# Loading the first 24 peer_u tiles of a two-layer PEER decoder without a turn on TensorE

## The chip, the cores and the metric

One core of a Trainium2 chip runs the whole kernel. The metric is the device time in microseconds from the start of the program to its end; less is better. Engines are called TensorE (PE in the profile; PEld is its weight load), VectorE (DVE), ScalarE (ACT), GpSimd (POOL) and SyncE (SP), which issues most transfers.

## The reference

Two layers, 256 tokens, 1024 channels. Each layer has a block of two token mixers and a PEER block; the change touches only the PEER block:

```python
q = (h @ w_pq).reshape(B, S, PEER_HEADS, 2, half)
s1 = jnp.einsum('bshd,hnd->bshn', q[..., 0, :], sub_keys[0])
s2 = jnp.einsum('bshd,hnd->bshn', q[..., 1, :], sub_keys[1])
v1, i1 = lax.top_k(s1, PEER_TOPK)
v2, i2 = lax.top_k(s2, PEER_TOPK)
cand = v1[..., :, None] + v2[..., None, :]
top, pos = lax.top_k(cand, PEER_TOPK)        # 16 of 16 x 16 pairs, with their indices idx
gates = jax.nn.softmax(top, axis=-1)
...
act = jax.nn.gelu(jnp.einsum('btd,bthkd->bthk', hb, u), approximate=False)   # u = peer_u[idx]
y = jnp.einsum('bthk,bthkd->btd', gb * act, peer_v[ib])
```

There are 8 heads, 128 keys on either side and so 16384 experts, of which each token and head uses 16. peer_u and peer_v have one row of 1024 channels for each expert.

## The kernel before

The kernel gathers nothing. It goes through all 16384 experts in 128 tiles of 128: for each it multiplies the peer_u tile with the modulated activations of all 256 tokens (hTh and hTl), applies gelu, multiplies by a gate that is zero where a token didn't choose the expert, and adds the products with the peer_v tiles in PSUM. So that float32 inputs keep their precision, each operand is split in a high part (wh, hTh; written by ScalarE) and a rest (wl, hTl), and each product is three: high by high, high by rest, rest by high. A peer_u tile is 8 channel blocks times 3, 24 products.

For a product on TensorE the channels must lie on the partitions, so a peer_u tile is turned. Line 124 names two ways, a kind for each tile:

- Kind u: four transfers (line 197) lay the tile down so that VectorE's block transpose (line 220, in `turn`) finishes the turn. ScalarE then writes the two halves of wh from it, and GpSimd subtracts to get those of wl (line 271, in `prep`).
- Kind x: four transfers (line 193) lay it down otherwise; TensorE turns it by eight transposes of 128x128 into PSUM (line 251, in `prep`), and ScalarE copies each of two banks twice: to wh, and back into the raw tile, from which GpSimd's subtraction reads.

Before, of the first 100 tiles every fourth (3, 7, 11, ...) is of kind x, 25 in a layer.

`take` hands out the tile that is prepared, starts a new transfer, prepares the next tile and turns the one after that. wh and wl have room for two tiles (HALVES), the raw tiles five buffers (RAW). For each tile `u_tile` (lines 1631 to 1643) calls `take`, issues the 24 products and, every second tile, the gelu of the pair before (`fin_u`).

Beside that runs the side work: a generator, `select`, that finds the top 16 and places the gates. After each tile `pull` (line 1650) advances it by a budget. The numbers that the generator yields, called points here, are the author's costs of its steps in microseconds of VectorE; `pull` subtracts them from a credit that it carries on, of at most two budgets, and a yield of None ends the pull of that tile. Every engine does its own work in the order of the program, so the budget sets how many operations of VectorE stand between two transposes. A tile of kind u gets 1.55 points, a tile of kind x 2.75.

The side work has three parts:
- The top-k: 17 steps of `zipped` (lines 1433 to 1438). A round, as it is called below, is one head and one half of the tokens: the key operations (ten, 0.2 points each) of round i interleaved with the candidate operations (0.0, twice 0.12, five times 0.18) of round i - 1. Before each, `scores(i + 1)` issues the score product (tile K) on TensorE and a copy of it on ScalarE; then ScalarE copies the high keys of round i - 1 into PSUM (vp, tile G), and the additions on VectorE (line 1404) read that copy.
- The tail of the selection (lines 1447 to 1498): indices of the chosen pairs, by comparisons and reductions over 2048 elements (lines 1473 to 1478) and many operations over 128.
- The gate placement (`place_gates`): 64 blocks of four tokens, each with two operations of 1024 elements on VectorE (lines 1507 and 1512), products on TensorE, and a product of the gates with the gelu values (line 1539).

After tile 125 `drain` (line 1653) empties what side work is left; then come the last two tiles of peer_u and the peer_v tiles.

Of the kernel before, what the change touches and what calls it, by code (L numbers as in the profile page):

```python
# [24 lines left out]
NK = 128  # L25
# [20 lines left out]
def trunk_kernel(ctx: ExitStack, tc: tile.TileContext, x, c, w_ada, b_ada, w_in, lb_logits, hg_norm_g,  # L46
# [74 lines left out]
            order.append((kind, w[l][k * P:(k + 1) * P, :], 0))  # L121


    uv_seq = [("x" if j % 4 == 3 and j < 100 else "u", j) for j in range(NK)] + [("v", j) for j in range(NK)]
    for l in range(DEPTH):
        if l == 0:

# [507 lines left out]
    def pull(sides, budget):  # L635

        credit[0] = min(credit[0] + budget, 2 * budget)
        for g in list(sides):
            while credit[0] > 0:
                try:  # L640
                    cost = next(g)
                except StopIteration:
                    sides.remove(g)
                    break
                if cost is None:
                    break
                credit[0] -= cost
                load["vector"] += cost
# [670 lines left out]
    def peer(l, hT):  # L1319
        with ExitStack() as es:  # L1320
# [11 lines left out]
            with ExitStack() as eu:  # L1332
# [227 lines left out]
                sides = []  # L1560
# [70 lines left out]
                def u_tile(j):  # L1631
                    h, lo = take(uv_seq[j][0])
                    if j % 2 == 0:
                        acts[0] = pst.tile([P, 2, S], F32, name="A")
                    ps = acts[0]
                    for k0 in (0, KC // 2):
                        kss = [(k, slice(k * P, (k + 1) * P)) for k in range(k0, k0 + KC // 2)]
                        products([(ps[:, j % 2], (h(ks), lo(ks)), (hTh[:, k], hTl[:, k]), k == 0, k == KC - 1)
                                  for k, ks in kss], 0)
                    if pend:  # L1640
                        fin_u(*pend.pop())
                    if j % 2 == 1:
                        pend.append((j - 1, ps))
# [3 lines left out]
                    f()  # L1647
                for i, (kind, j) in enumerate(uv_seq[:nu]):
                    u_tile(j)
                    pull(sides, 1.55 + 1.2 * (kind == "x"))  # L1650
                if pend:
                    fin_u(*pend.pop())
                drain(sides)
# [111 lines left out]
    for l in range(DEPTH):  # L1765
        hT = mixers(l, hT)
        hT = peer(l, hT)
# [27 lines left out]
```

## Time and profile before

| | us |
|---|---|
| median of 3 runs (lowest to highest) | 2228.16 (2227.01 to 2228.52) |
| the profiled execution | 2227.97 |
| its span, first to last instruction | 2226.2 |
| TensorE busy | 2117.0 |
| VectorE busy | 1819.4 |
| ScalarE busy | 1164.5 |
| GpSimd busy | 1063.8 |

The span is 1.8 us shorter than the execution. Busy times are averages over stages that differ: what binds a stage is read from a table by stretches, and who waits for whom from the waits of the stretch. Times of single operations in a timeline are durations; on VectorE one operation can start before the one ahead of it has ended, so the cost of an operation in a full stretch is read from the distance of two starts. In a chain or a timeline, rows of equal kind that follow one another are merged and counted (x24).

### The profile page before, as it was taken

To read this page: it belongs to the slowest core of one execution; us is meant where nothing else is said; L and a number is where in the kernel's file an instruction comes from. 1 tells how busy PE (TensorE), PEld (TensorE's weight loads), DVE (VectorE), ACT (ScalarE), POOL (GpSimd) and SP (SyncE) were. 2 spreads that over 40 slices of the span, in tenths; PEclk is the share of its full clock that TensorE was granted. 3 is DMA by queue.
4 is the path that set the end of the run, shared out by engine and by line. 5 is a ranking of instruction groups with operands and counts; after the bars stand their busy time and mean duration, and the time that the engine had idled before them with its cause. 6 is when DMAs were issued, how large, how long until landed. Compare 5 with 4: busy or idle time off the path is not lost.

```text
span 2226.2 us, 42039 instructions
## 1 busy us (share of the span) xinstructions
PE 2117.0 (95%) x14484; PEld 1928.0 (87%) x14484; DVE 1819.4 (82%) x3296; ACT 1164.5 (52%) x2443; POOL 1063.8 (48%) x784
## 2 busy tenths in 40 slices
PE   5799899999999999999989998998999999999998
PEld 5789799999999977888779887998999999788886
DVE  7887979999999578888887658789999985766675
ACT  3446555545554545555545465555555545555562
POOL 4656637887778621000044534578877783300001
PEclk8899999999999999999999999999999999999999
DMA  8646567676665678888844335676766556666662
GB/s 281 193 133 221 167 132 158 149 151 146 143 147 146 186 251 270 282 283 284 298 153 146 120 103 146 149 155 142 154 146 145 147 159 192 220 196 191 197 226 87
DMA packets 448718, 400.30 MB, mean 180 GB/s; under 512 B 234576, under 2 KB 395896, under 8 KB 448504
## 3 DMA queue, kind: packets, MB, share of 16 engines
q1 hardware_dynamic: 446760, 392.33, 62.5%
q0 software_dynamic: 1408, 4.23, 0.6%
q8 instruction: 114, 1.87, 0.3%
q10 hardware_dynamic: 336, 1.06, 0.1%
q14 instruction: 100, 0.82, 0.1%
HBM read 396.46 MB, written 1.05 MB: 179 GB/s over the span
## 4 chain that ended last, share of the span: by engine, by line
PE 69%; DVE 15%; DMA 5%; issue 3%; ACT 3%; POOL 2%; SPq 1%; POOLq 0%; ACTq 0%; DVEq 0%
PE Y L61 27%; PE A L61 25%; PE T L61 7%; PE G L61 3%; DMA raw<-in_peer_u_dram 3%; POOL wl L271 2%; PE hs L61 2%; DVE wl L271 2%; PE ss L61 2%; PE T L251 2%; DMA raw<-in_peer_v_dram 1%; DVE qk L857 1%; DVE o L1512 1%; SPq L197 1%; DVE e L843 1%
## 5 line engine op out<-in xcount | busy, mean ns | idle before, releaser
L271 POOL TENSOR_TENSOR wl<-raw,wh 128x512 fp32r<-128x512 f32 x663 | 925.7, 1421 | 662.0 <-ACT wh L58 587.3
L58 ACT ACTIVATE wh<-raw 128x512 fp32r<-128x512 f32 x1088 | 627.7, 622 | 206.8 <-PE A L61 59.0
L61 PE MATMUL A<-hTh,wh 128*128 128x256 f32 x2080 | 538.5, 291 | 2.7 <-ACT wh L58 2.6
L61 PE MATMUL A<-hTl,wh 128*128 128x256 f32 x2080 | 521.0, 283 | 0.0
L61 PE MATMUL Y<-wh,o 128*128 128x512 f32 x1776 | 478.1, 391 | 0.5 <-DVE o L521 0.5
L271 DVE TENSOR_TENSOR wl<-raw,wh 128x512 fp32r<-128x512 f32 x525 | 379.7, 764 | 64.0 <-ACT wh L58 46.4
L61 PEld LDWEIGHTS A<-hTh,wh 128*128 128x128 f32 x2080 | 397.8, 191 | 4.7 <-ACT wh L58 4.0
L61 PEld LDWEIGHTS A<-hTl,wh 128*128 128x128 f32 x2080 | 398.7, 192 | 0.7
L61 PEld LDWEIGHTS Y<-wh,o 128*128 128x128 f32 x1776 | 332.6, 188 | 70.0 <-DVE o L521 0.9
L61 PE MATMUL A<-hTh,wl 128*128 128x256 f32 x2080 | 336.2, 284 | 13.5 <-POOL wl L271 13.4
L61 PEld LDWEIGHTS A<-hTh,wl 128*128 128x128 f32 x2080 | 286.9, 192 | 17.6 <-POOL wl L271 17.6
L61 PE MATMUL Y<-wl,o 128*128 128x512 f32 x888 | 276.3, 391 | 5.2 <-DVE wl L271 5.0
L220 DVE STREAM_TRANSPOSE raw<-raw 128x1024 f32<-128x1024 f32 x206 | 252.8, 1233 | 3.2 <-DMA raw<-in_peer_u_dram 2.7
L58 ACT ACTIVATE o<-buf 128x256 fp32r<-128x256 f32 x228 | 95.0, 417 | 272.6 <-PE Y L61 272.6
L521 DVE TENSOR_TENSOR o<-buf,o 128x256 fp32r<-128x256 f32 x228 | 100.7, 442 | 140.2 <-ACT o L58 140.2
L61 PEld LDWEIGHTS Y<-wl,o 128*128 128x128 f32 x888 | 167.1, 188 | 44.0 <-DVE wl L271 9.5
L58 ACT ACTIVATE buf<-G 128x128 f32<-128x128 f32 (+6 forms) x236 | 53.8, 273 | 202.7 <-PE G L61 202.7
L1507 DVE TENSOR_TENSOR o<-iT,iota_t 128x1024 f16<-128x1024 f16 x128 | 159.5, 1246 | 0.0
L570 POOL TENSOR_TENSOR x<-x,buf 128x1024 f32<-128x1024 f32 x1 | 2.4, 2392 | 280.9 <-DVE x L567 280.9
L1512 DVE TENSOR_TENSOR o<-gT,o 128x1024 f16<-128x1024 f16 x128 | 131.3, 1025 | 4.4
L61 PE MATMUL T<-hTh,wh 128*128 128x256 f32 x512 | 133.8, 293 | 0.0
L61 PE MATMUL T<-hTl,wh 128*128 128x256 f32 x512 | 130.4, 287 | 0.0
(496 smaller groups left out, 3212.6 us busy)
## 6 DMA issues: line engine op xcount, KB each, us to landing
raw<-in_peer_u_dram SPq DMA_DIRECT2D x1024, 128.0 KB, 3.5
raw<-in_peer_v_dram SPq DMA_DIRECT2D x256, 512.0 KB, 4.6
raw<-in_w_in_dram SPq DMA_DIRECT2D x88, 512.0 KB, 4.7
raw<-in_w_ada_dram SPq DMA_DIRECT2D x78, 512.0 KB, 4.9
raw<-in_w_o_dram SPq DMA_DIRECT2D x16, 512.0 KB, 3.5
raw<-in_w_pq_dram SPq DMA_DIRECT2D x64, 128.0 KB, 2.9
qk<-in_w_ada_dram SPq DMA_DIRECT2D x10, 512.0 KB, 3.7
e<-in_w_ada_dram SPq DMA_DIRECT2D x8, 512.0 KB, 6.0
```

Source lines behind the costliest of these rows:

```text
L58: nc.scalar.activation(o, i, f, **kw)
L61: nc.tensor.matmul(o, a, b, start=start, stop=stop, **kw)
L197: nc.sync.dma_start(dst[32 * b:32 * b + 32], src[b])
L220: nc.vector.transpose(t, t)
L251: nc.tensor.transpose(banks[s][:, q], t[:, (4 * s + q) * P:(4 * s + q + 1) * P], ident)
L271: eng.tensor_sub(lo, src, h.bitcast(F32))
L521: nc.vector.tensor_sub(lo, src, h.bitcast(F32))
L570: nc.gpsimd.tensor_mul(xt[tt], xt[tt], last[0])
L843: eng.tensor_sub(ev[:, :, :hn], mid, bv[:, :, :hn])
L857: nc.vector.tensor_mul(tv[:, :, hn:], nodes(qT, n)[:, :, hn:], ev[:, :, hn:])
L1507: nc.vector.tensor_tensor(o.rearrange("p a u n v -> p (a u) n v"), iT[:, b].rearrange("p a (u v) -> p (a u) v", v=2)[:, :, None] .to_broad ...
L1512: nc.vector.tensor_mul(og.rearrange("p u a n v -> p (u a) n v"), gT[:, b * nu:(b + 1) * nu].rearrange("p u a v -> p (u a) v")[:, :, None] ...
```

## The change

The 24 first tiles of each layer's peer_u are all of kind u, so the six of kind x among them (3, 7, 11, 15, 19, 23) become kind u: loaded by the transfers of line 197, turned by VectorE, written to wh by ScalarE from SBUF. And the budget of each of the 24 is 1.75, in place of 1.55 or 2.75. From tile 24 on nothing is changed.

```diff
-    uv_seq = [("x" if j % 4 == 3 and j < 100 else "u", j) for j in range(NK)] + [("v", j) for j in range(NK)]
+    uv_seq = [("x" if j % 4 == 3 and 24 <= j < 100 else "u", j) for j in range(NK)] + [("v", j) for j in range(NK)]
...
                 for i, (kind, j) in enumerate(uv_seq[:nu]):
                     u_tile(j)
-                    pull(sides, 1.55 + 1.2 * (kind == "x"))
+                    pull(sides, 1.75 if j < 24 else 1.55 + 1.2 * (kind == "x"))
```

## Rows read from the trace of the kernel before

**Rows 1.** The page: the span, and the busy time of each engine with its share of the span and its instructions.

```profile
span 2226.2 us, 42039 instructions
...
PE 2117.0 (95%) x14484; PEld 1928.0 (87%) x14484; DVE 1819.4 (82%) x3296; ACT 1164.5 (52%) x2443; POOL 1063.8 (48%) x784
```

**Rows 2.** The table by stretches (us from the span's start): length of the stretch, then busy time and instructions of each engine, the granted TensorE clock, the share of the DMA engines and what they moved. The first stretch holds tiles 0 to 23 of layer 0, the second the end of the top-k and the tail; the row that begins with 1416.78 is the first stretch of layer 1, and the last one the gate placement of layer 0.

```profile
core 0: us, PE busy (x) PEld busy (x) DVE busy (x) ACT busy (x) POOL busy (x), PEclk, DMA share, GB/s
323.08:402.88 79.80, 79.80 (x653) 78.98 (x652) 69.38 (x369) 45.88 (x101) 60.25 (x48) 1.00 0.72 158
402.88:472.17 69.29, 62.52 (x504) 60.25 (x504) 68.28 (x107) 35.77 (x66) 59.01 (x39) 1.00 0.65 144
...
1416.78:1496.58 79.80, 79.80 (x652) 78.98 (x652) 69.38 (x369) 45.88 (x101) 60.23 (x48) 1.00 0.72 157
...
472.17:720.00 247.83, 244.59 (x2262) 238.88 (x2262) 241.90 (x350) 133.30 (x346) 193.03 (x137) 1.00 0.63 147
```

**Rows 3.** The chain that ended last, through the first 24 tiles of layer 0: start, length, engine and tile. A is a tile's product (24 a tile), K a score product of the top-k, T on L251 the turn of an x tile.

```profile
323.08 5.75 PE A L61 x48
328.84 0.43 PE K L61 x2
329.27 0.87 PE T L251 x8
...
335.89 0.43 PE K L61 x2
336.33 2.87 PE A L61 x24
...
400.01 8.62 PE A L61 x72
```

**Rows 4.** Groups by line in tiles 0 to 23 of layer 0: instructions, busy time, mean ns of one, idle time of the engine before them and what ended it; VectorE, then ScalarE, then GpSimd.

```profile
L220 DVE STREAM_TRANSPOSE raw<-raw 128x1024 f32<-128x1024 f32 x17 | 21.0, 1238 | 0.0
...
L1404 DVE TENSOR_TENSOR buf<-G,buf 128x64 f32<-128x64 f32 (+1 forms) x28 | 5.8, 206 | 10.4 <-ACT G L58 10.4
...
L58 ACT ACTIVATE wh<-raw 128x512 fp32r<-128x512 f32 x36 | 20.7, 625 | 2.2 <-issue 1.4 <-PE A L61 0.4 <-POOL wl L271 0.4
L58 ACT ACTIVATE raw<-T 128x512 f32<-128x512 f32 x12 | 7.3, 605 | 0.0
L58 ACT ACTIVATE wh<-T 128x512 fp32r<-128x512 f32 x12 | 7.2, 602 | 7.0 <-PE T L251 6.9
...
L271 POOL TENSOR_TENSOR wl<-raw,wh 128x512 fp32r<-128x512 f32 x48 | 61.0, 1299 | 19.7 <-ACT wh L58 11.6 <-ACT raw L58 5.5 <-DVE buf L1412 1.8
```

**Rows 5.** ScalarE's longest wait in tiles 0 to 23 of layer 0: who waited for whom, us in all, times, longest.

```profile
ACT buf L58 <- PE K L61: 22.8, 13, 3.1
```

**Rows 6.** The timeline of VectorE in layer 0: start, length, operation, and in brackets the idle time before it. A round of the top-k begins at its first L1404; the last row is the first operation of the tail.

```profile
329.80 0.23 DVE L1404 TENSOR_TENSOR buf<-G,buf 128x64 f32<-128x64 f32 x1 [2.41 <-ACT G L58]
...
330.22 1.23 DVE L220 STREAM_TRANSPOSE raw<-raw 128x1024 f32<-128x1024 f32 x1
331.37 0.17 DVE L1404 TENSOR_TENSOR buf<-G,buf 128x48 f32<-128x48 f32 x1
...
336.86 0.22 DVE L1404 TENSOR_TENSOR buf<-G,buf 128x64 f32<-128x64 f32 x1 [1.03 <-ACT G L58]
...
338.57 1.24 DVE L220 STREAM_TRANSPOSE raw<-raw 128x1024 f32<-128x1024 f32 x1
...
341.66 0.22 DVE L1404 TENSOR_TENSOR buf<-G,buf 128x64 f32<-128x64 f32 x1
...
400.54 0.23 DVE L1404 TENSOR_TENSOR buf<-G,buf 128x64 f32<-128x64 f32 x1 [2.15 <-ACT G L58]
...
409.74 0.34 DVE L1404 TENSOR_TENSOR buf<-G,buf 128x64 f32<-128x64 f32 x2
...
412.94 0.53 DVE L1448 COPY buf<-buf 128x8 f32<-128x8 f32 x1
```

**Rows 7.** The tail of layer 0: four operations of VectorE's timeline; the group of the first kind in 402.88 to 472.17; and TensorE's longest waits in that stretch.

```profile
414.24 0.22 DVE L1457 TENSOR_SCALAR buf<-buf 128x128 uint32<-128x128 uint32 x1
414.38 0.22 DVE L1460 CAST buf<-buf 128x128 f16<-128x128 uint32 x1
...
415.67 0.99 DVE L1457 TENSOR_SCALAR buf<-buf 128x128 uint32<-128x128 uint32 x1
416.58 1.33 DVE L1460 CAST buf<-buf 128x128 f16<-128x128 uint32 x1
...
L1457 DVE TENSOR_SCALAR buf<-buf 128x128 uint32<-128x128 uint32 x4 | 2.7, 686 | 0.0
...
PEld A L61 <- POOL wl L271: 8.4, 9, 1.7
...
PE A L61 <- POOL wl L271: 6.6, 9, 1.5
```

**Rows 8.** The end of peer_u in layer 0: a piece of the chain, 384 products in a row.

```profile
723.38 46.12 PE A L61 x384
```

**Rows 9.** The block transposes in the whole trace, and SP's issues of peer_u transfers in tiles 0 to 23 of layer 0 (L197: kind u, L193: kind x): count, then ns min/median/max, first and last start.

```profile
L220 DVE STREAM_TRANSPOSE raw<-raw x206: 1195/1234/1255, 312.1 to 1852.3; 128x1024 f32<-128x1024 f32 x103
...
L197 SPq DMA_DIRECT2D raw<-in_peer_u_dram x72: 311/430/1734, 322.9 to 401.8; - x72
L193 SPq DMA_DIRECT2D raw<-in_peer_u_dram x24: 384/582/1369, 329.8 to 398.5; - x24
```

## The prediction

> **What bounds the kernel now.** I read four views in this order: the page, to see which engine is full; the table by stretches, to see where it is not; the chain of waits through the 24 tiles, to see what stands between their products; the timeline of VectorE, to see what it waits for there.
>
> The page has TensorE busy for 95% of the span and VectorE for 82% [rows 1]. By stretches, the first 24 tiles of peer_u in layer 0 (323.08 to 402.88 us) are full of TensorE work: 79.80 of 79.80 us, at a granted clock of 1.00 (2.4 GHz); VectorE works 69.38, GpSimd 60.25, ScalarE 45.88 [rows 2]. Layer 1 repeats them within 0.02, so I work out one layer and double it. Next comes the tail of the selection (402.88 to 472.17, call it the tail). There VectorE is full (68.28 of 69.29) and TensorE is not (62.52). In the gate placement behind it (472.17 to 720) both are nearly full: TensorE 244.59, VectorE 241.90 of 247.83. Then 16 tiles run with no side work, on TensorE alone [rows 2, 8].
>
> In the chain the 24 tiles are a string of TensorE pieces: 2.87 us for the 24 products of a tile, 0.43 for a score product of the top-k (13 of them), 0.87 for the eight transposes of an x tile (6 of them) [rows 3]. 24 x 2.87 + 13 x 0.43 + 6 x 0.87 = 79.7, the stretch. VectorE's idle time in it, 10.4 us, has a single cause: the first candidate operation of a top-k round waits for a ScalarE copy [rows 4], which stands in ScalarE's queue behind the copy of the next round's score, which waits for the score product behind a whole tile on TensorE (22.8 us of ScalarE waits, 13 times [rows 5]).
>
> **The change, part by part, for one layer.**
>
> *Removed from TensorE*: 6 x 0.87 = 5.2 us of transposes, all on the path [rows 3]. If nothing else came to bind, that would be the gain.
>
> *Removed from ScalarE*: of each x tile's four copies out of PSUM (0.60 each), two; the other two become the usual 0.62 from SBUF [rows 4]. 6 x 1.2 = 7.2 us of an engine with 34 us to spare: nothing on the path, though the copies that VectorE waits for stand in a shorter queue.
>
> *Added to VectorE*: six block transposes; one lasts 1.24 and the next operation starts 1.15 behind its start [rows 4, 6]. 6 x 1.15 = 6.9 us. Their duration hardly varies (1.20 to 1.26 in the whole trace [rows 9]), so no bound on either side is needed.
>
> *Moved*: side work. Before, the 24 tiles give 18 x 1.55 + 6 x 2.75 = 44.4 points; after, 24 x 1.75 = 42.0. The 2.4 points come later.
>
> *DMAs*: four per tile before and after; those of an x tile held SP's queue for 582 ns each at the median, those of the others for 430 [rows 9]. SP gains a little; nothing waits there in this stretch. I cost it at nothing; were its cover gone, the bound would be a saving of 6 x 4 x 0.15 = 3.6 us of queue.
>
> *GpSimd*: 48 subtractions of 1.30 us, unchanged [rows 4]. 2.6 us a tile fit under 2.87.
>
> Is VectorE fast enough? I walk it through by the points. A round (one head, one half of the tokens) costs 10 x 0.2 + 1.14 = 3.14 points. Adding up the budgets puts the score products before behind tiles 1, 3, 4, 6, 8, 10, 11, 13, 15, 16, 18, 20, 22, just where the chain has them; after they come behind 1, 3, 5, 6, 8, 10, 12, 14, 15, 17, 19, 21, 22. A round can start 0.54 behind the end of the score product in front of it [rows 3, 6]. From the start of round 2 (329.80) to that of round 14 (400.54) are 70.74 us: 12 rounds, 16 transposes of 1.15 = 18.4, and 10.4 - 2.4 = 8.0 idle [rows 4, 6]. That leaves 3.70 a round; the one round from 336.86 to 341.66 with one transpose gives 4.80 - 1.15 = 3.65.
>
> After: round 2 starts at 329.80 as well (its score product is still behind tile 1). Round 3 would be reached at 335.8 and released at 336.0, round 4 reached at 342.0 and released at 342.1; from then on VectorE arrives later than its release, by 1.5 us at round 5 and about 3.4 at round 14. So nearly all of the idle time is used up: 12 x 3.70 + 21 x 1.15 + 0.3 = 68.9, and round 14 starts at 398.7, only 1.9 earlier. On to the point where the tail starts with the transpose of tile 29 done: two rounds 7.4, the last half round 2.05 (409.74 to 412.94 less one transpose), four transposes 4.6: 412.75; before, the same state is at 412.94 + 1.15 = 414.1 [rows 6]. **VectorE gains 1.3 us, where TensorE would gain 5.2**: the bound of the 24 tiles passes from TensorE to VectorE, and TensorE's lead runs out in the tail, where it already waits (8.4 us of weight loads and 6.6 of products, overlapping, for wl [rows 7]).
>
> A part comes back, because the deferred points spread the same side work over more tiles. Adding up the budgets again: tail from tile 26 to 44 before (18 tiles) and 27 to 46 after (19); gate placement 44 to 111 (67) and 46 to 114 (68). The 16 bare tiles of 2.88 [rows 8] become 13. A tile that moves under side work costs VectorE 1.15 there and saves TensorE 2.87 at the end, up to 1.72 net where VectorE binds. In the tail, if the 2 x 1.3 of GpSimd count instead, it is 0.27; I take 1.72, as VectorE is full there. In the gate placement it lies between 0 (TensorE full) and 1.72; I take 0.6, a third, as TensorE is the fuller of the two.
>
> Before these trades, a rule against the change: the Trainium skill, "VectorE: DVE Perf Modes", section "Rules for kernel authors", says to turn 128x128 on TensorE where PSUM will do as the destination. The row has eight such turns at 0.87 us of a full engine against 1.15 of one with 10.4 idle. By the 390 ns that the same page gives for one turn, the six x tiles would hold TensorE for 18.7 us (an estimate); by the chain it is 5.2, and the chain stands.
>
> Sum for a layer: -1.3 - 1.7 - 0.6 = -3.6, between -1.6 (1.3 + 0.27) and -4.7 (1.3 + 1.72 + 1.72). For two: **-7.2**, from -3.2 to -9.4. The profiled execution took 2227.97 us, 1.8 more than its span; 2227.97 - 7.2 = 2220.8, and as the median of the runs is 0.2 above it, I forecast **2221.0**. About 0.2% (4.5 us) is what a measurement of this kernel can tell from no change.
>
> **The rivals.**
>
> *TensorE keeps the bound.* VectorE's lateness is absorbed by tiles turned ahead (a tile is turned two ahead of its use), and the tail, thinner by a tile, gives it back. For it: TensorE has no gap in the stretch although VectorE now and then starts a transpose 2 us into a tile. Against: the tail has no slack on VectorE. 2 x 5.2 = 10.4: 2217.8.
>
> *Nothing is gained.* VectorE still waits at the start of rounds, as ScalarE's copies come in the order of the program; 1.3 us more idle than the 0.3 that I walked uses up the gain of the first stage, and in the tail and gate placement the extra tiles are worth 0.27 and 0. For it: all eight waits today are of this kind. Against: after round 4 each release lies ahead of VectorE's arrival. -0.3 a layer: 2227.6.
>
> *Slower: the small operations of the tail meet GpSimd.* In the tail an integer shift of 128x128 takes 0.22 us at 414.24 and 0.99 at 415.67, the cast behind it 0.22 and 1.33, the long ones while GpSimd is inside a subtraction [rows 7]. There are some 20 such operations a layer, and the change shifts them by a tile or two against the subtractions. A meeting costs 1.1 us of the engine that binds. From 6 more meetings a layer the kernel is slower by what can be measured (6 x 1.1 - 3.6 = 3.0, doubled 6.0): 2234. For it: the trace has both durations side by side. Against: the shifts of this kind now average 0.69, so as many could get shorter. The Trainium skill, "SBUF — State Buffer", section "SBUF: two separate sides", calls the port pair of the two engines an exclusive lock held for a whole instruction; the trace agrees with the durations of these two lines, and the transposes, one input each, show no such spread [rows 7, 9].
>
> **How the numbers follow.** Forecast 0.52, TensorE keeps the bound 0.14, nothing gained 0.22, slower 0.12. The forecast's own span (2218.6 to 2224.8) reaches past 2223.7, where a gain can no longer be told, by about a tenth of its chance. Faster: 0.46 + 0.14 = 0.60; same: 0.06 + 0.22 = 0.28; slower: 0.12. The range takes in the first three cases: 2216.5 to 2227.8.
>
> **What would show each step.** In the profile after: eight fewer transposes for each of 12 x tiles (L251 from 400 to 304) and 12 more stream transposes (L220 from 206 to 218); TensorE's time for the 24 tiles 74 to 76 us with VectorE at 96% or more and its waits for the ScalarE copy under 3 us a layer; TensorE waiting earlier and longer in the front of the tail; 13 bare tiles instead of 16 at the end of peer_u. I am wrong if VectorE still idles by more than 3 us in the 24 tiles, if a round costs another time than 3.70, or if the tail's small operations change their mean by more than 0.2 us.

## The result, and the profile after

The changed kernel takes 2214.15 us (median of 4 runs, 2213.49 to 2216.07), the kernel before on the same chip 2227.75: 13.6 us less, ratio 0.994 (95%: 0.9923 to 0.9958). Measured again (run e9 below) it was 2215.84 against 2228.51, ratio 0.9946 (0.9933 to 0.996). The forecast was 2221.0 with a range from 2216.5: the sign was right, the gain nearly twice the forecast's, and the time lies outside the range. The profiled execution took 2214.01 us, 13.96 less than that of before.

The page after, answering to [rows 1]; then the counts of the two kinds of turn (ns min/median/max, first and last start), the second answering to [rows 9]:

```profile
span 2212.2 us, 41797 instructions
...
PE 2104.2 (95%) x14388; PEld 1915.7 (87%) x14388; DVE 1822.3 (82%) x3310; ACT 1151.8 (52%) x2417; POOL 1072.3 (48%) x784
```

```profile
L251 PE MATMUL T<-ident,raw x304: 270/273/277, 403.2 to 1750.8; 128*128 128x128 f32 x152
...
L220 DVE STREAM_TRANSPOSE raw<-raw x218: 1194/1232/1251, 312.0 to 1838.7; 128x1024 f32<-128x1024 f32 x109
```

The edit did what it says: 96 of TensorE's transposes fewer, 12 block transposes more. TensorE's busy time fell by 12.8 us; 12 x 0.87 = 10.4 of it are those transposes.

Where the gain lies is read from the start of each tile (its first product on TensorE, counted off in 24s from the trace), relative to the start of tile 0. Gain over before, in us:

| | at tile 24 | at tile 30 | at tile 46 | at tile 100 | at tile 112 | end of peer_u |
|---|---|---|---|---|---|---|
| layer 0 | 5.2 | 5.3 | 7.6 | 8.2 | 8.2 | 6.5 |
| layer 1 | 5.2 | 5.3 | 7.6 | 8.5 | 8.8 | 7.05 |

Together 13.6 of the 13.96. The table by stretches, cut at those starts (tiles 0 to 23, 24 to 45, 46 to 99, 100 to 127 of layer 0; columns as in [rows 2]), first of after, then the same second stretch of before:

```profile
core 0: us, PE busy (x) PEld busy (x) DVE busy (x) ACT busy (x) POOL busy (x), PEclk, DMA share, GB/s
322.62:397.38 74.76, 74.76 (x604) 74.02 (x603) 73.12 (x370) 41.39 (x90) 59.60 (x48) 1.00 0.61 165
397.38:474.22 76.84, 71.55 (x584) 69.60 (x583) 73.81 (x128) 38.60 (x72) 68.22 (x46) 1.00 0.71 155
474.22:670.95 196.73, 195.37 (x1819) 191.09 (x1818) 192.01 (x277) 109.68 (x290) 156.32 (x109) 1.00 0.65 146
670.95:759.83 88.88, 85.49 (x746) 83.63 (x745) 70.93 (x100) 43.40 (x91) 74.90 (x55) 1.00 0.61 163
```

```profile
402.71:481.90 79.19, 72.42 (x593) 70.11 (x591) 78.01 (x117) 39.45 (x74) 68.35 (x45) 1.00 0.70 151
```

In the 24 tiles TensorE is still full, 74.76 of 74.76, while VectorE has gone from 69.4 of 79.8 [rows 2] to 73.1 of 74.8, 98%. In tiles 24 to 45 TensorE's idle time (length less busy) fell from 6.77 to 5.29, instead of rising. The chain of waits through the 24 tiles is the string of [rows 3] without its six pieces of transposes, and at the end of peer_u 304 products (12.7 tiles) run bare where 384 did [rows 8]:

```profile
322.97 5.75 PE A L61 x48
328.72 0.43 PE K L61 x2
329.16 5.75 PE A L61 x48
...
394.24 0.43 PE K L61 x2
...
726.14 36.74 PE A L61 x304
```

VectorE's wait for the ScalarE copy is down to 1.6 us, from 10.4 [rows 4], and ScalarE's for the score products to 16.2, from 22.8 [rows 5] (waits of the 24 tiles: us in all, times, longest). Behind them VectorE's timeline shows the transposes of tiles 24, 25 and 30, with the first operation of the tail among them:

```profile
ACT buf L58 <- PE K L61: 16.2, 13, 2.8
...
DVE buf L1404 <- ACT G L58: 1.6, 3, 1.3
```

```profile
394.55 1.24 DVE L220 STREAM_TRANSPOSE raw<-raw 128x1024 f32<-128x1024 f32 x1
...
397.70 1.24 DVE L220 STREAM_TRANSPOSE raw<-raw 128x1024 f32<-128x1024 f32 x1
...
411.23 0.15 DVE L1448 COPY buf<-buf 128x8 f32<-128x8 f32 x1
...
412.56 1.24 DVE L220 STREAM_TRANSPOSE raw<-raw 128x1024 f32<-128x1024 f32 x1
```

Before, the transposes of tiles 24 and 30 stood here (same view):

```profile
396.79 1.23 DVE L220 STREAM_TRANSPOSE raw<-raw 128x1024 f32<-128x1024 f32 x1
...
420.67 1.23 DVE L220 STREAM_TRANSPOSE raw<-raw 128x1024 f32<-128x1024 f32 x1
```

One quantity explains the 24 tiles; call it the **head start** of a tile: from the end of its transpose on VectorE to its first product on TensorE. For tile 24 it was 402.71 - 398.02 = 4.7 us before and is 397.38 - 395.79 = 1.6 after. For tile 30 it was 422.74 (its first product) - 421.90 = 0.8, with TensorE waiting inside that tile, and is 417.36 - 413.80 = 3.6. Counted from the start of tile 0 (322.73 before, 322.62 after), VectorE gained only 2.1 us on tile 24's transpose where TensorE gained 5.2; the difference came out of the head start. On tile 30's transpose it gained 8.0: this one now stands 1.3 us behind the first operation of the tail, where it stood 7.7 us behind it.

### The profile page after: what moved, and what is told of

Its sections match the earlier page's. It is cut to its first block, busy times and chain, and to the rows that moved or that the text cites. A ratio compares the mean times of both kernels' runs of the same rounds, so it can differ in the third digit from the quotient of the medians.

```text
span 2212.2 us, 41797 instructions
## 1 busy us (share of the span) xinstructions
PE 2104.2 (95%) x14388; PEld 1915.7 (87%) x14388; DVE 1822.3 (82%) x3310; ACT 1151.8 (52%) x2417; POOL 1072.3 (48%) x784
## 3 DMA queue, kind: packets, MB, share of 16 engines
HBM read 396.46 MB, written 1.05 MB: 180 GB/s over the span
## 4 chain that ended last, share of the span: by engine, by line
PE 66%; DVE 18%; DMA 5%; issue 4%; ACT 3%; POOL 3%; SPq 1%; POOLq 0%; ACTq 0%; DVEq 0%
PE Y L61 26%; PE A L61 24%; PE T L61 6%; PE G L61 3%; DMA raw<-in_peer_u_dram 3%; DVE wl L271 2%; POOL wl L271 2%; PE ss L61 2%; PE hs L61 2%; DMA raw<-in_peer_v_dram 1%; PE T L251 1%; DVE raw L220 1%; DVE qk L857 1%; SPq L197 1%; DVE e L843 1%
## 5 line engine op out<-in xcount | busy, mean ns | idle before, releaser
L58 ACT ACTIVATE wh<-raw 128x512 fp32r<-128x512 f32 x1112 | 640.3, 622 | 228.5 <-POOL wl L271 62.2
L220 DVE STREAM_TRANSPOSE raw<-raw 128x1024 f32<-128x1024 f32 x218 | 266.9, 1230 | 3.9 <-DMA raw<-in_peer_u_dram 3.8
L58 ACT ACTIVATE buf<-G 128x128 f32<-128x128 f32 (+4 forms) x232 | 52.6, 271 | 195.2 <-PE G L61 195.2
L1507 DVE TENSOR_TENSOR o<-iT,iota_t 128x1024 f16<-128x1024 f16 x128 | 151.1, 1180 | 0.0
L1512 DVE TENSOR_TENSOR o<-gT,o 128x1024 f16<-128x1024 f16 x128 | 137.0, 1070 | 4.4
```

Of the source, the lines that this page charges most:

```text
L58: nc.scalar.activation(o, i, f, **kw)
L220: nc.vector.transpose(t, t)
L1507: nc.vector.tensor_tensor(o.rearrange("p a u n v -> p (a u) n v"), iT[:, b].rearrange("p a (u v) -> p (a u) v", v=2)[:, :, None] .to_broad ...
L1512: nc.vector.tensor_mul(og.rearrange("p u a n v -> p (u a) n v"), gT[:, b * nu:(b + 1) * nu].rearrange("p u a v -> p (u a) v")[:, :, None] ...
```

## The experiments

"Gain" below is against before on the same chip, between medians; the interval of the ratio is 2 to 4 us wide on either side. The last column is what the two layers of peer_u gain in the traces, counted as in the table above. It repeats better: two traces of the changed kernel give 13.6 and 13.7, two of e5's kernel 14.6 both. The points are those given in the 24 tiles.

| run | x tiles among the 24 | points | median us | gain | ratio (95%) | peer_u in the traces |
|---|---|---|---|---|---|---|
| before | 6 | 44.4 | 2227.75 to 2228.7 | | |  |
| changed | 0 | 42.0 | 2214.15 | 13.6 | 0.994 (0.9923 to 0.9958) | 13.6 |
| e9, changed | 0 | 42.0 | 2215.84 | 12.7 | 0.9946 (0.9933 to 0.996) | 13.7 |
| e1 | 0 | 44.4 uneven | 2219.31 | 9.4 | 0.9958 (0.9941 to 0.9975) | 6.6 |
| e2 | 6 | 42.0 | 2224.24 | 4.5 | 0.998 (0.997 to 0.9989) | 4.4 |
| e3 | 0, six unturned | 42.0 | 2212.72 | 16.0 | 0.9931 (0.9915 to 0.9948) | 16.0 |
| e4 | 0 | 37.2 | 2218.06 | 10.6 | 0.9953 (0.9936 to 0.997) | 8.1 |
| e5 | 0 | 39.6 | 2212.28 | 15.9 | 0.9934 (0.9917 to 0.995) | 14.6 |
| e10, as e5 | 0 | 39.6 | 2213.25 | 15.3 | 0.9933 (0.9919 to 0.9947) | 14.6 |
| e11 | 0 | 40.8 | 2212.32 | 16.2 | 0.9931 (0.9918 to 0.9945) | 13.7 |
| e6 | 0 | 44.4 even | 2222.41 | 5.7 | 0.9975 (0.9965 to 0.9985) | 5.8 |
| e7 | 0, two turned thrice | 42.0 | 2224.53 | 3.6 | 0.9982 (0.9973 to 0.9992) | 3.4 |
| e8 | 0 | 42.0, then 0.25 less a tile | 2215.44 | 12.7 | 0.9942 (0.9926 to 0.9959) | 13.0 |

The theory after the result was that TensorE keeps the bound, so that the transposes removed count in full. The rival was the forecast's own: VectorE binds, and the deferred points bring the rest.

**e1: the kinds alone.** The budgets stay where they were, by tile number.

```diff
-                    pull(sides, 1.75 if j < 24 else 1.55 + 1.2 * (kind == "x"))
+                    pull(sides, 2.75 if j % 4 == 3 and j < 100 else 1.55)
```

> The first 24 tiles are of kind u, but every tile keeps the budget that it had before (2.75 for tiles 3, 7, 11, ..., 1.55 for the others), so no side work is deferred. TensorE theory (the removed transposes count in full, 5.2 us a layer; what the changed kernel gains beyond that, 1.4 us a layer, comes from the deferred points): 10.4 us under before, about 2217.4, TensorE without a gap up to tile 26, 16 bare tiles at the end as before. VectorE theory (VectorE is the bound from tile 6 to the end of the gate placement, and the gain is its idle time used up): 6 x 1.15 = 6.9 us of transposes against at most 10.4 us of idle time, 3.5 a layer at most: 2220.8 or later.

2219.31, between the two. The trace sides with the rival: TensorE has gaps in the 24 tiles (stretch below, answering to the first of after), the gain is 3.7 at tile 24, 2.8 at tile 30 and 4.0 at the end (3.5, 2.6 and 2.6 in layer 1). The gaps sum to 0.6 us where 1.5 are lost: a product lasts 0.28 us while the next starts 0.12 behind it, so part of a wait counts as busy. With the points left in place VectorE does bind.

```profile
322.44:398.71 76.27, 75.66 (x605) 74.26 (x603) 74.87 (x382) 41.43 (x90) 59.51 (x48) 1.00 0.59 160
```

**e2: the budget alone.** The x tiles stay; the 24 tiles get 1.75.

```diff
-    uv_seq = [("x" if j % 4 == 3 and 24 <= j < 100 else "u", j) for j in range(NK)] + [("v", j) for j in range(NK)]
+    uv_seq = [("x" if j % 4 == 3 and j < 100 else "u", j) for j in range(NK)] + [("v", j) for j in range(NK)]
```

> Kinds as before (x tiles 3, 7, ..., 23 stay), only the budget of the first 24 tiles is 1.75, so 2.4 points come later. TensorE theory: the 5.2 us of transposes stay, the thinner tail of the selection gives 1.4 us a layer: 2225.0. VectorE theory: in the 24 tiles VectorE idles longer by 2.8 us a layer, which it needs later, and the tail and gates get three more tiles, each worth 2.87 - 1.15: within 1 us a layer of before, 2226 to 2229.

2224.24, a little faster than either theory had it. Nothing is gained up to tile 24 (TensorE is as full as before), 1.1 by tile 30, 3.6 by tile 46, and 1.7 is given back between tiles 112 and 116: 2.5 and 1.9 at the end of the layers. TensorE's idle time in tiles 24 to 45 is 75.62 - 71.00 = 4.6 instead of 6.8:

```profile
404.01:479.63 75.62, 71.00 (x585) 69.45 (x583) 72.34 (x122) 38.08 (x72) 67.33 (x45) 1.00 0.70 154
```

Between medians the gains of e1 and e2, 9.4 + 4.5 = 13.9, make up the change's. In the traces they don't: 6.6 + 4.4 = 11.0 in peer_u, against 13.6. At tile 24 the kinds alone gain 3.7 and the budget alone nothing, both together 5.2: the deferred points make the room in which the added turns cost TensorE nothing.

**e3: the turns left out.** The six tiles of a layer are loaded and prepared as kind u, but not turned; their transposes, 6.9 us of VectorE a layer, are left out of the computation.

```diff
-                order.append((kind, peer_u[l].rearrange("(a r j) (b f) -> j b r a f", a=4, j=NK, b=4)[j], 4))
+                order.append(("ut" if j < 24 and j % 4 == 3 else kind, peer_u[l].rearrange("(a r j) (b f) -> j b r a f", a=4, j=NK, b=4)[j], 4))
```

> The changed kernel without the six added block transposes: tiles 3, 7, ..., 23 of peer_u are loaded as kind u and left unturned, so these six tiles of each layer are multiplied in a wrong order of channels; all else is the same. TensorE theory: VectorE's 6.9 us a layer were hidden, so nothing changes by more than 1.5 us a layer: 2211 to 2214. VectorE theory: they were on the path, and up to 6.9 us a layer come off: 2200 to 2205.

2212.72, as the TensorE theory had it; in its trace the layers gain 7.75 and 8.2, only 1.2 more each than the changed kernel, and the 24 tiles take the same 74.76 us. The six turns cost 1.2 of their 6.9 us; 5.1 of them run in time in which VectorE is idle without them (6.7 us idle here, 1.6 after):

```profile
321.57:396.33 74.76, 74.76 (x604) 74.02 (x603) 68.06 (x359) 40.78 (x90) 60.29 (x49) 1.00 0.63 167
```

**e4: the budget without the special value**, 24 x 1.55.

```diff
-                    pull(sides, 1.75 if j < 24 else 1.55 + 1.2 * (kind == "x"))
+                    pull(sides, 1.55 + 1.2 * (kind == "x"))
```

> The changed kernel with a budget of 1.55 in the first 24 tiles, 37.2 points, so 7.2 points are deferred in place of 2.4: by the sum of the budgets the tail of the selection begins at tile 29 in place of 27, the side work ends at tile 117 in place of 114. TensorE theory: the 24 tiles take the same time; TensorE's idle time in the tail shrinks by up to another 1.5 us a layer and VectorE idles in the 24 tiles again: 2211 to 2214. VectorE theory: 4.8 points of about 1.17 us leave the stretch where VectorE has idle time and go where it has none, against three more tiles under side work worth up to 1.7 each: 0 to 1 us a layer slower, 2214 to 2216.

2218.06: slower than either theory had it. It leads by 5.8 at tile 24, 6.3 at tile 30 and 8.0 at tile 100, and gives back 4.2 behind tile 112. The side work now runs to tile 117, and from tile 100 on VectorE has to turn every tile: TensorE idles 91.37 - 86.67 = 4.7 us there (second row), where it idled 3.4 in the changed kernel and 3.2 before. Between tiles 30 and 46 its lead shrinks by 0.8, where the changed kernel's grows by 2.3; in tiles 24 to 45 TensorE idles 79.45 - 72.25 = 7.2 us (first row), more than before.

```profile
397.01:476.46 79.45, 72.25 (x583) 69.88 (x582) 73.19 (x152) 39.29 (x76) 65.67 (x45) 1.00 0.65 146
671.35:762.72 91.37, 86.67 (x762) 84.57 (x761) 76.22 (x110) 43.74 (x94) 76.05 (x55) 1.00 0.57 159
```

These four together gave a new theory: VectorE's margin in the 24 tiles is thin, and points taken out of them pay until the side work ends too late. The next four test it.

**e5 and e6: one step of the budget down and up.**

```diff
-                    pull(sides, 1.75 if j < 24 else 1.55 + 1.2 * (kind == "x"))
+                    pull(sides, 1.65 if j < 24 else 1.55 + 1.2 * (kind == "x"))
```

> The changed kernel with a budget of 1.65 in the first 24 tiles: 39.5 points. Its tail of the selection begins at tile 28 (27 with 1.75, 29 with 1.55), the side work ends at tile 115. Theory of the thinner tail (each deferred point takes idle time of TensorE out of the tail): at least as fast as the changed kernel, 14 to 16 us under before. Theory of the place (1.75 is good because of where its tail's turns on TensorE and its x tiles fall, so that more points deferred don't gain): between 1.75 (13.6 under before) and 1.55 (10.6 under), or anything up to 2 us beside that.

2212.28, 15.9 under before, as the theory of the thinner tail had it. In layer 0 TensorE leads by 9.3 at tile 46 and by 11.4 at tile 112, and loses 3.7 by tile 120. In tiles 24 to 45 it idles 75.54 - 71.58 = 4.0 us, 5.3 in the changed kernel:

```profile
396.95:472.49 75.54, 71.58 (x587) 69.92 (x585) 70.14 (x142) 39.35 (x74) 68.94 (x45) 1.00 0.69 154
```

One step up:

```diff
+                    pull(sides, 1.85 if j < 24 else 1.55 + 1.2 * (kind == "x"))
```

> The changed kernel with a budget of 1.85 in the first 24 tiles: 44.4 points as in the kernel before and in the run with the kinds only, but even. By the sum of the budgets the tail begins at tile 26 and the side work ends at tile 111, as before. Margin theory (with 2.4 points fewer VectorE just keeps up with TensorE in the 24 tiles, with the old 44.4 points it doesn't, and what it is late is lost to TensorE at the front of the tail): as with the kinds only, 8.5 to 10.5 us under before. If it is the uneven budgets (2.75 and 1.55) that made VectorE late: 12 to 13.5 under before.

2222.41: slower than the changed kernel, as the margin theory had it, but by more (5.7 under before, expected 8.5 to 10.5). In peer_u the traces of e1 and e6 are nearer to each other than their medians, 6.6 and 5.8. With 44.4 points, the number of before, the 24 tiles take 77.39 us, and tile 24's transpose stands at 397.93, counted from the start of tile 0 2.7 later than after. Its head start is 400.73 - 399.17 = 1.6, and it has been between 1.0 and 1.9 since tile 8: no tile is turned early any more. VectorE waits for nothing but 1.8 us in this stretch, and it sets the pace.

```profile
323.34:400.73 77.39, 76.60 (x604) 74.44 (x603) 75.57 (x387) 41.51 (x90) 59.48 (x48) 1.00 0.59 159
```

```profile
397.93 1.24 DVE L220 STREAM_TRANSPOSE raw<-raw 128x1024 f32<-128x1024 f32 x1
```

**e7: four more turns.** Tiles 8 and 16 are turned three times (two of them cancel): 4.6 us more of VectorE a layer.

```diff
-            if kind == "u":
-                nc.vector.transpose(t, t)
+            if kind in ("u", "u3"):
+                for _ in range(3 if kind == "u3" else 1):
+                    nc.vector.transpose(t, t)
```

> The changed kernel with tiles 8 and 16 of peer_u in each layer turned three times by VectorE (which leaves what one turn leaves): 4 x 1.15 = 4.6 us more of VectorE a layer inside the 24 tiles, budgets and all else the same. Margin theory (VectorE has next to nothing left there): TensorE stalls by 3.5 to 4.6 us a layer before or in the front of the tail, 7 to 9 us slower than the changed kernel, so 4.5 to 6.5 under before. TensorE theory (VectorE's work there is hidden): under 1.5 us a layer, 10.5 to 13.5 under before.

2224.53, 3.6 under before: slower still than the margin theory had it. Both layers lose 5.1 us against the changed kernel and never recover it: 1.9 by tile 12 and 5.0 by tile 20, each right behind a tile with extra turns. TensorE now waits for VectorE by way of ScalarE: ScalarE waits for keys that VectorE writes behind the three turns, and the copy to wh stands behind that in ScalarE's queue (waits of the 24 tiles; L1387 is L1386 of the other runs):

```profile
PE A L61 <- ACT wh L58: 2.9, 3, 1.4
...
PEld A L61 <- ACT wh L58: 3.8, 3, 1.8
...
ACT G L58 <- DVE buf L1387: 5.3, 3, 2.8
```

So below the changed kernel's load a microsecond of VectorE costs about 0.2 (1.2 of 6.9, e3), above it about 1.1 (5.1 of 4.6, e7). The extra turns come in two lumps; e6's 2.4 points more, which are spread evenly, cost TensorE 2.6 and 2.3 us at tile 24.

**e8: points taken out of the tail instead.**

```diff
-                    pull(sides, 1.75 if j < 24 else 1.55 + 1.2 * (kind == "x"))
+                    pull(sides, 1.75 if j < 24 else (1.3 if j < 48 else 1.55) + 1.2 * (kind == "x"))
```

> The changed kernel with 0.25 points less for each of tiles 24 to 47 (1.30 and 2.50), so that its tail runs from tile 27 to 49 in place of 46 and the side work ends at tile 118. Theory of the thinner tail: TensorE's idle time between tiles 24 and 46 falls from 5.3 us a layer to 3 or less, 2 us a layer faster: 16 to 18 us under before. Theory of the place: that idle time changes by under 1 us either way, 12 to 15 under before.

2215.44, 12.7 under before: no gain over the changed kernel, as the theory of the place had it. In tiles 24 to 45 TensorE's idle time falls from 5.3 to 74.95 - 70.85 = 4.1 (first row), where the theory of the thinner tail wanted 3 and that of the place a change under 1. In layer 0 the lead reaches 12.7 at tile 100, and 5.7 of it is gone by tile 120; TensorE idles 92.86 - 87.36 = 5.5 us behind tile 100. Points put off are only moved: of the 4.4 us by which this kernel is ahead of the changed one at tile 100 it keeps 0.45 in layer 0, and layer 1 ends 1.0 behind.

```profile
397.79:472.74 74.95, 70.85 (x581) 69.23 (x580) 70.71 (x123) 38.81 (x72) 68.14 (x46) 1.00 0.74 157
666.93:759.79 92.86, 87.36 (x770) 85.07 (x769) 79.19 (x115) 43.95 (x95) 76.60 (x55) 1.00 0.56 155
```

**e9, e10 and e11: three budgets side by side**, on one chip: the changed kernel, e5 again, and 1.70.

> The changed kernel itself, on the same chip as the two that follow. Its first measurement was 13.6 us under before; by the times of peer_u in its trace (6.5 and 7.05 us shorter) it should be 13 to 14.5 under.

> The changed kernel with a budget of 1.65, once more, beside the changed kernel on one chip. By the traces peer_u is 7.7 and 6.9 us shorter than before, 14.6 in all, 1.1 better than with 1.75. If that is so: 0.5 to 2 us faster than the changed kernel. If the 2.3 us between the first two measurements came from the chips: as with 1.75 within 0.5 us.

```diff
-                    pull(sides, 1.75 if j < 24 else 1.55 + 1.2 * (kind == "x"))
+                    pull(sides, 1.7 if j < 24 else 1.55 + 1.2 * (kind == "x"))
```

> The changed kernel with a budget of 1.70, 40.8 points. If the time follows the points (too many: VectorE late in the 24 tiles; too few: side work past tile 112, where no x tile relieves VectorE): between 1.65 and 1.75 or up to 1 us better than either, 13.5 to 16.5 under before. If single placements decide: up to 3 us beside that.

2215.84, 2213.25 and 2212.32. The last two can't be told apart; their medians lie 2.6 and 3.5 us under the changed kernel's, but the intervals against before overlap. In the traces peer_u is 1.0 us shorter than the changed kernel's with 1.65, both times, and within 0.2 of it with 1.70. In e11 tile 24 has a head start of 397.98 - 395.36 = 2.6, and its neighbours back to tile 10 have the same within 0.3: VectorE and TensorE run at one pace, and the 1.3 us that left no gap at tile 25 of the changed kernel show that there is some to spare.

```profile
394.14 1.22 DVE L220 STREAM_TRANSPOSE raw<-raw 128x1024 f32<-128x1024 f32 x1
```

## Why the prediction was right and wrong

**The step that failed** is the first term of the sum, as the prediction put it: "VectorE gains 1.3 us, where TensorE would gain 5.2: the bound of the 24 tiles passes from TensorE to VectorE, and TensorE's lead runs out in the tail". TensorE gained the 5.2 (6 x 0.87) in full and had it still at tile 30. Three things were wrong with the 1.3:

- Its comparison was at the same state of the side work ("the point where the tail starts with the transpose of tile 29 done"). TensorE doesn't wait for the side work, it waits for transposes, and with 42.0 points instead of 44.4 there is less side work ahead of each. Tile 30 was turned 8.0 us earlier: 2.8 of them are VectorE's gain at the same state, the other 5.2 are operations of the tail that now come behind the transpose. e1 and e6, which have 44.4 points, gain 2.2 to 2.8 at tile 30: only with the points in place does the forecast's mechanism appear. The 2.4 points were credited to the tail and the gate placement alone.
- It took VectorE's lateness as TensorE's. Before, tile 24 was turned 4.7 us ahead of use; after, 1.6. These 3.1 us were a store that the stretch could use up once, and it did, just: the head start falls from 3.3 at tile 4 to 1.6 at tile 24 and 1.3 at tile 25, without a gap on TensorE.
- The walk itself was a little slow. The idle time was right (1.6 us, of which 0.3 behind the first wait, as walked). A round with two transposes in it takes 5.92 us from start to start (below), so a round costs 5.92 - 2.30 = 3.62, not 3.70: 1.1 us over fourteen. By the forecast's own measure the tail was reached at 411.23 with tile 29 turned, not at 412.75: VectorE gained 2.9 (2.8 counted from tile 0), not 1.3.

```profile
352.78 0.21 DVE L1404 TENSOR_TENSOR buf<-G,buf 128x64 f32<-128x64 f32 x1
...
358.70 0.21 DVE L1404 TENSOR_TENSOR buf<-G,buf 128x64 f32<-128x64 f32 x1
```

**The later terms** (1.7 for the thinner tail, 0.6 for the gate placement) had the right sign, as e2 shows for the tail (its idle time 4.6 in place of 6.8 from the deferred points alone), and their sum was near: from tile 30 to the end of peer_u the layers gained 1.2 and 1.8 instead of 2.3. The parts were not. Up to tile 46 it was 2.3. The gate placement then gave 0.7 to 1.2 up to tile 112, and the next four tiles took 1.7 back: three fewer run bare, as forecast (304 products against 384), and there the side work that had been put off is paid for. From tile 46 on the layers lost 1.05 and 0.5, where the bounds were 0 and a gain of 1.72. So that the sum was near is luck in part. Nor does the tail follow the points as the term has it: TensorE's idle time in tiles 24 to 45 is 5.3 with 42.0 and 40.8 points, 4.0 with 39.6, but 7.2 with 37.2 (e4).

**The rivals.** "TensorE keeps the bound" (0.14) is what happened in the 24 tiles, for the reason given for it (tiles turned ahead); its objection, that the tail has no slack on VectorE, fell because the same change thins the tail. It priced only the 10.4 us, and the thinning added the rest. "Nothing is gained" needed VectorE to keep waiting at the start of rounds; that wait fell from 10.4 to 1.6 us. "Slower: the small operations" did not come: their durations changed line by line, their sum hardly (below). The range failed because no case put the first rival together with the later terms: 2 x 5.2 and 2 x 2.3 make 15.0, or 2213.2.

**The signs named in the prediction**: L251 at 304, L220 at 218, 13 bare tiles, 74.76 us for the 24 tiles, VectorE at 98% and its wait at 1.6 us all came as written or within it. "TensorE waiting earlier and longer in the front of the tail", the sign of the failed step, hardly did: between tiles 24 and 30 its idle time was 0.5 us instead of 0.3 (rows below, before and after), but over the tail it was 5.3 instead of 6.8. Of the signs of being wrong, two came: a round took 3.62 instead of 3.70, and single lines of the tail changed their mean (last section).

```profile
402.71:422.74 20.03, 19.70 (x162) 19.05 (x160) 19.72 (x67) 12.38 (x23) 13.69 (x11) 1.00 0.68 159
```

```profile
397.38:417.36 19.98, 19.49 (x163) 19.08 (x161) 19.67 (x80) 12.74 (x24) 15.66 (x13) 1.00 0.74 166
```

The rule weighed there, from the Trainium skill, "VectorE: DVE Perf Modes", section "Rules for kernel authors" (turn 128x128 on TensorE), is decided here by which engine has room: the turns of six tiles cost 5.2 us on TensorE and 1.2 on VectorE (e3).

**What stays open**: why e4's lead shrinks between tiles 30 and 46. Between tiles 32 and 38 it isn't VectorE's transposes: the lead shrinks by 1.9 us there, while those of tiles 33 to 38 end 5.5 to 8.1 us ahead of use. In tiles 24 to 45 TensorE waits longer for wl, which GpSimd writes (rows below, e4 and then the changed kernel); what makes GpSimd late isn't shown.

```profile
PE A L61 <- POOL wl L271: 7.0, 10, 1.5
```

```profile
PE A L61 <- POOL wl L271: 4.9, 7, 1.3
```

Nor is it shown that e5 and e11 are faster than the changed kernel by all of their medians' distance, 2 to 3.5 us: in their traces the two layers of peer_u together are only 1.1 and 0.2 us shorter. The rest would lie outside peer_u, which the change doesn't touch and which varies: between the traces of e5 and e10, one and the same kernel, it differs by 2.9 us (1331.1 and 1334.0).

## What to carry to other kernels

Compare two engines by when one delivers what the other waits for, item by item, not by when each reaches the same state of some other work that is interleaved with it. An engine at 98% of a stretch need not bind it: what decides is the head start that it has at the beginning, what it loses per tile, and how many tiles the stretch has. Moving work to the slacker engine and thinning the other work put in front of it belong together; look for the budget at which both run at one pace (of those tried, 1.65 a tile has the shortest peer_u), and ask where the work put off will land.

## What the runs showed of the hardware

**The small operations of the tail** changed their durations line by line. Groups of before, then of after, in the same part of the tail (count, busy us, mean ns; the first of before is in [rows 7]):

```profile
L1460 DVE CAST buf<-buf 128x128 f16<-128x128 uint32 x4 | 3.1, 774 | 0.0
...
L1467 DVE SCALAR_TENSOR_TENSOR buf<-buf 128x128 f32<-128x128 f16 x4 | 2.0, 531 | 0.1
...
L1463 DVE SCALAR_TENSOR_TENSOR buf<-buf 128x128 f16<-128x128 uint32 x2 | 1.7, 842 | 0.0
...
L1469 DVE SCALAR_TENSOR_TENSOR buf<-buf 128x128 f16<-128x128 f32 x2 | 0.5, 266 | 0.0
```

```profile
L1467 DVE SCALAR_TENSOR_TENSOR buf<-buf 128x128 f32<-128x128 f16 x4 | 3.0, 778 | 0.0
L1469 DVE SCALAR_TENSOR_TENSOR buf<-buf 128x128 f16<-128x128 f32 x2 | 2.5, 1264 | 0.1
...
L1463 DVE SCALAR_TENSOR_TENSOR buf<-buf 128x128 f16<-128x128 uint32 x2 | 1.7, 836 | 0.0
...
L1460 DVE CAST buf<-buf 128x128 f16<-128x128 uint32 x4 | 1.5, 374 | 0.0
...
L1457 DVE TENSOR_SCALAR buf<-buf 128x128 uint32<-128x128 uint32 x4 | 0.9, 216 | 0.0
```

L1457 fell from 686 to 216 ns and L1469 rose from 266 to 1264, a factor of nearly five, while the five sum to 10.0 us before (with the 2.7 of L1457) and 9.6 after. Four of the five means moved by more than the 0.2 us that the prediction named as a sign of error; over all sixteen operations the mean went from 0.63 to 0.60, and the forecast slowdown didn't come.

**TensorE's clock**, among the tiles of peer_u, fell in two of the traces: once in e1, in the tail of layer 0, and once in e6, in that of layer 1. The table by stretches of 1 us, e1:

```profile
420.00:421.00 1.00, 0.87 (x8) 0.66 (x6) 1.00 (x1) 1.00 (x4) 1.00 (x1) 1.00 0.83 200
421.00:422.00 1.00, 0.00 (x0) 0.00 (x0) 0.97 (x2) 1.00 (x4) 1.00 (x1) 1.00 0.06 11
422.00:423.00 1.00, 0.64 (x4) 0.64 (x5) 1.00 (x1) 0.55 (x2) 1.00 (x2) 0.83 0.04 8
423.00:424.00 1.00, 1.00 (x6) 1.00 (x6) 1.00 (x2) 0.00 (x0) 1.00 (x1) 0.50 0.03 8
...
425.00:426.00 1.00, 1.00 (x7) 1.00 (x6) 1.00 (x1) 0.85 (x2) 1.00 (x2) 0.50 0.20 32
426.00:427.00 1.00, 1.00 (x10) 1.00 (x10) 1.00 (x2) 0.00 (x0) 1.00 (x2) 0.96 0.97 153
```

TensorE did nothing for some 1.5 us, began again, and then ran at 0.50 (1.2 GHz) for some 3.4 us, with 6 products in a microsecond in place of 10. In the changed kernel a pause at 430 to 432 (0.27 and 0.53 busy) left the clock at 1.00. What it cost was soon made up: e1's lead was 2.80 at tile 30, 2.11 at tile 32 and 2.80 at tile 34.
